# Attention values as the stationary operand, two key heads in column halves, in a hybrid trunk on one core

## The chip, the core and the metric

The kernel runs on one core of a Trainium2 chip. The metric is the device time of one execution in microseconds (us). The time of a kernel is the median of its runs; the profile is one further execution, with timestamps for the instructions of each engine. Engines: TensorE (PE) multiplies matrices, VectorE (DVE), ScalarE (ACT) and GpSimd (POOL) do elementwise work, and SyncE (SP) issues the DMAs. Matmuls read SBUF and write PSUM, which has eight banks of 128 partitions by 512 fp32 columns here.

## The reference

A trunk of two layers on 256 tokens of width 1024, all in fp32. Each layer has a feed-forward half step, a mixer, a second half step and a gated embedding. The mixer normalises x, multiplies it by one wide matrix `w_in`, and gives the columns to an mLSTM (four heads) and to a sliding-window attention (eight query heads on two key heads, 64 wide), whose outputs meet in two gated products:

```python
z = u @ w_in[i]
hA = mlstm_chunkwise(...)
yA = (jax.nn.sigmoid(mo) * rmsnorm(hA, ml_out_norm[i])) @ w_a[i]
pr = jnp.exp(logits - m)
denom = jnp.sum(pr, axis=-1, keepdims=True) + jnp.exp(sink - m)
hB = jnp.einsum('bnkgqs,bnskd->bnqkgd', pr / denom, vv)
yB = hB @ w_b[i]
mixed = jax.nn.sigmoid(ga) * yA + jax.nn.sigmoid(gb) * yB
x = x + mixed @ w_out[i]
```

## The kernel before

The tokens are two tiles of 128, called t = 0 and t = 1. Every weight is read once from HBM, in units of up to 128 x 2048 (`load_next`): one DMA into `raw` on SP's queue, then for each half of the unit a cast to `hi` on ACT (L203) and the rest `lo = raw - hi` on DVE (L204). Units are loaded three ahead of their use. A product of activations and weights is three matmuls of 512 columns each (`mm_unit`, L231 lo, L232 hi with the activations' lo, L233 hi), and the activations are split into `hi` and `lo` the same way (`split_evac`, L247 and L248 in the rows).

TensorE works in the order in which the code is written; the instructions of the other engines are put in order by a scheduler when the program is built. `stream` takes one unit, multiplies it with both token tiles (12 matmuls for each in `w_in`), and calls `tick()` after each tile. `tick()` advances every side task, a Python generator, by one step: so the attention, the mLSTM and the transposes are written between the units of a product. The counts W_... say how many steps a task waits.

The mixer multiplies `w_in` in nine pieces, sq, if, mqk, mv, mo, ga0, ga1, gb0, gb1 (`project`). Beside the last four of these run:

- `swa_logits` and `swa_part`: logits L, their exponentials (L694), the row sums rs and the reciprocal rinv (L699) of the softmax; then the transpose of L to PT. t = 0 has one part with all eight heads, t = 1 has two parts of four heads (`_1_0` and `_1_4`), as it sees 256 keys in two blocks kt.
- A transpose of this kind (`turn`) doesn't use TensorE: DVE transposes blocks of 32 x 32 (L264), a DMA writes the result to a scratch in HBM (L270, `scr`), a second one reads it back in another order (L274, `back`), and a copy puts it in its place (for PT: ACT at L709 for the first block of a part, DVE at L711 for the others). The `back` tile has two buffers, and PT, hb and ha all use them.
- the product of PT with the values `vsw` (L721), into `ov`: PT is the stationary operand (128 keys x 128 tokens), the values (128 keys x 64) move; one small matmul for each head and each kt, 8 for t = 0 and 16 for t = 1. The output has tokens on partitions. `hb = ov * rinv` (L729), then hb takes the same way over HBM to have its channels on partitions, and is split into `abT[t][1]`, which the rows call abT_1.
- `ml_mix` and `ml_out`: products st of the mLSTM's queries and keys (L807, L815; row halves of the array side by side), E times st on DVE (L811, L819), num (L838 for t = 0, L840 and L841 for t = 1) from E and its values, its denominator dd and r (L844, L845), ha = num * r (L846), squares on ACT (L850), vn and rn (L852, a power on POOL), the norm (L856), a sigmoid gate (ACT L881, DVE L862), and the way over HBM to `abT[t][0]`, abT_0.

After gb1 `drain()` lets every task end, and for each half n of the output columns `stream` multiplies abT_1 by `w_b` (yb) and abT_0 by `w_a` (ya): 24 matmuls each, t = 0 first. `by_cols` gives `w_b`'s half as one DMA: row 128 k + p of the matrix on partition p, k = 0 to 3, which matches hb's channels in order.

Of the kernel before, what the change touches and what calls it, by code (L numbers as in the profile page):

```python
# [8 lines left out]
F32 = mybir.dt.float32  # L9
# [5 lines left out]
P = 128  # L15
# [13 lines left out]
SWKV = 2  # L29
# [28 lines left out]
W_OV = 2  # L58
W_HB = 1
W_ST = 2  # L60
# [5 lines left out]
def trunk_kernel(ctx: ExitStack, tc: tile.TileContext, a: dict, out: bass.AP):  # L66
# [14 lines left out]
    def bank(name):  # L81
        return psum.tile([P, 512], F32, tag="bank", name=name)
# [34 lines left out]
    def by_cols(w, rows, cols, name):  # L117
# [13 lines left out]
        ]  # L131

    def by_rows(w, rows, name):
        return [
            (f"{name}_{k}", k, 2, [w[k * P : (k + 2) * P, :]], D) for k in range(0, rows // P, 2)
        ]
# [29 lines left out]
    for i in range(DEPTH):  # L166
        specs.extend(ffn_specs(a["ffn1_wi"][i], a["ffn1_wo"][i], f"f1{i}"))
        for z, cols in Z.items():
            specs.extend(by_cols(a["w_in"][i], D, cols, f"z{i}_{z}"))
        for n in range(2):  # L170
            cols = [(512 * n, 512 * (n + 1))]
            specs.extend(by_cols(a["w_b"][i], 512, cols, f"wb{i}_{n}"))
            specs.extend(by_cols(a["w_a"][i], 512, cols, f"wa{i}_{n}"))
        specs.extend(by_rows(a["w_out"][i], D, f"wout{i}"))
        specs.extend(ffn_specs(a["ffn2_wi"][i], a["ffn2_wo"][i], f"f2{i}"))
        specs.extend(by_rows(a["w_ple"][i], PDIM, f"wple{i}"))
        specs.extend(by_rows(a["w_ple_gate"][i], D, f"pg{i}"))
    loaded = deque()

    def load_next(between=()):  # L180
# [14 lines left out]
        else:  # L195
            c0 = 0
            for s in srcs:
                w = s.shape[1]
                nc.sync.dma_start(rv[:, :, c0 : c0 + w], s.rearrange("(k p) c -> p k c", p=P))
                c0 += w  # L200
# [316 lines left out]
    def mix_in(pool, i, xn, finish):  # L517
# [127 lines left out]
        def swa_logits(t):  # L645
# [6 lines left out]
            nh = SWQ if t == 0 else SWQ // SWKV  # L652
            parts = []
            for h0 in range(0, SWQ, nh):
                nmp = f"{i}_{t}_{h0}"
# [17 lines left out]
            for h0, L, mx in parts:  # L673
                gen = swa_part(t, h0, nh, L, mx)
                spawn(gen)
                advance(gen)

        def swa_part(t, h0, nh, L, mx):
            part = slice(h0, h0 + nh)
# [18 lines left out]
            rinv = stat("rinv")  # L698
            nc.vector.reciprocal(rinv, rs)  # L699
            for _ in range(W_PT):  # L700
                yield
# [11 lines left out]
            for _ in zip(*[turn_p(kt, j0) for kt in range(t + 1) for j0 in range(0, nh, 4)], strict=True):  # L713
                yield
            for _ in range(W_OV):
                yield
            ov = bank(f"ov{nmp}")[:, 0 : nh * HD]
            for j in range(nh):
                g = (h0 + j) // 4
                for kt in range(t + 1):  # L720
                    nc.tensor.matmul(  # L721
                        ov[:, j * HD : (j + 1) * HD],
                        PT[:, kt, j, :],
                        vsw[kt][:, g * HD : (g + 1) * HD],
                        start=kt == 0,
                        stop=kt == t,
                    )
            hb = work.tile([P, nh * HD], F32, tag="sg", name=f"hb{nmp}")
            nc.vector.tensor_tensor(  # L729
                heads(hb, HD), heads(ov, HD), rinv[:, :, None].broadcast_to([P, nh, HD]), op=ALU.mult  # L730
            )
            for _ in range(W_HB):
                yield
            ks = slice(h0 * HD // P, (h0 + nh) * HD // P)
            hi, lo = (part[:, ks, :] for part in abT[t][1])
            yield from back_split(blocks(hb), hi, lo, f"hb{nmp}")

# [313 lines left out]
```

## Time and profile before

| what | before |
|---|---|
| median of three runs | 1118.13 us (1116.99 to 1119.06) |
| the profiled execution, its own time | 1118.42 us |
| its span | 1116.6 us |
| DVE TENSOR_TENSOR lo_f, 128x1024, 176 times | 207.5 us busy, mean 1216 ns |
| PE matmuls h_f of 128x512, L232 | 352, 137.8 us busy, mean 392 ns |

The span runs from the first instruction to the last. A row of the timeline has the start in us, the duration in us, the engine, the line, the operation, output <- inputs, the shapes (output <- input), and how many instructions it stands for; a bracket says how long the engine sat idle ahead of it and what it waited for. Matmuls overlap in the pipeline, so their pace is read from start to start and not from the duration.

### The profile page before, as it was taken

The numbers are of one execution on the slowest core, as the hardware profiler recorded it, in microseconds if no ns is written. First come the engines' busy times: TensorE is split into PE (matmuls) and PEld (weight loads), VectorE is DVE, ScalarE is ACT, GpSimd is POOL, SyncE is SP. The second block draws the span as 40 slices with busy tenths as digits, with TensorE's granted clock in tenths as the row PEclk, the third lists the DMA queues.
The fourth block names the chain that finished last, engine by engine and source line by source line (L and its number), as shares of the span: only waits on it lengthen the run. The fifth ranks groups of instructions, "written<-read, shape, count | busy, mean of one in ns | idle before, by whom it ended". The sixth has DMA issues, their size and how long they took to land.

```text
span 1116.6 us, 13467 instructions
## 1 busy us (share of the span) xinstructions
PE 1104.3 (99%) x5096; PEld 913.7 (82%) x5096; DVE 756.7 (68%) x958; ACT 585.7 (52%) x848; POOL 29.6 (3%) x30
## 2 busy tenths in 40 slices
PE   8999999999999999999999999999999999999998
PEld 6788888878878888888888888888787888888887
DVE  5775655689787576656676666556987777667563
ACT  5543544668545444444664454446784454444442
POOL 1000000010000000000000000001000000000000
PEclk9999999999999999999999999999999999999999
DMA  7888766778764867766657776666777557777551
GB/s 252 282 268 255 258 212 191 244 229 264 241 212 156 274 228 254 247 202 221 215 164 246 261 231 224 214 206 211 254 249 243 198 185 245 244 238 247 194 207 38
DMA packets 170337, 251.30 MB, mean 225 GB/s; under 512 B 18472, under 2 KB 70816, under 8 KB 170272
## 3 DMA queue, kind: packets, MB, share of 16 engines
q1 hardware_dynamic: 170272, 250.44, 68.4%
q8 instruction: 40, 0.66, 0.2%
q14 instruction: 25, 0.20, 0.1%
HBM read 227.59 MB, written 22.83 MB: 224 GB/s over the span
## 4 chain that ended last, share of the span: by engine, by line
PE 80%; DVE 11%; DMA 4%; issue 2%; ACT 2%; POOL 1%; SPq 0%; DVEq 0%
PE h_f L232 14%; PE h_f L231 14%; PE h_f L233 14%; PE acc_f_o L232 7%; PE acc_f_o L233 7%; PE acc_f_o L231 7%; DMA back_PT<-scr_PT 2%; PE acc_wout L233 1%; PE acc_wout L231 1%; PE acc_wout L232 1%; PE acc_pg L233 1%; PE acc_pg L231 1%; PE acc_pg L232 1%; DVE lo_z_ga L204 1%; DVE inq_PT L264 1%
## 5 line engine op out<-in xcount | busy, mean ns | idle before, releaser
L204 DVE TENSOR_TENSOR lo_f<-raw_f,hi_f 128x1024 fp32r<-128x1024 f32 (+1 forms) x176 | 207.5, 1216 | 85.2 <-ACT hi_f L203 84.9
L203 ACT CAST hi_f<-raw_f 128x1024 fp32r<-128x1024 f32 (+1 forms) x178 | 176.5, 1038 | 143.8 <-PE h_f L233 88.1
L204 DVE TENSOR_TENSOR lo_f_o<-raw_f_o,hi_f_o 128x1024 fp32r<-128x1024 f32 x88 | 104.2, 1219 | 71.9 <-ACT hi_f_o L203 71.8
L232 PE MATMUL h_f<-hi_f,xT_f_0l 128*128 128x512 f32 x352 | 137.8, 392 | 2.2 <-DVE xT_f_0l L248 2.2
L231 PE MATMUL h_f<-lo_f,xT_f_0h 128*128 128x512 f32 x352 | 138.5, 393 | 0.2 <-POOL lo_f L204 0.2
L233 PE MATMUL h_f<-hi_f,xT_f_0h 128*128 128x512 f32 x352 | 137.7, 391 | 0.0
L231 PE MATMUL h_f<-lo_f,xT_f_1h 128*128 128x512 f32 x352 | 137.2, 390 | 0.5 <-DVE lo_f L204 0.4
L232 PE MATMUL h_f<-hi_f,xT_f_1l 128*128 128x512 f32 x352 | 137.0, 389 | 0.0
L233 PE MATMUL h_f<-hi_f,xT_f_1h 128*128 128x512 f32 x352 | 136.9, 389 | 0.0
L203 ACT CAST hi_f_o<-raw_f_o 128x1024 fp32r<-128x1024 f32 x88 | 88.0, 1048 | 90.0 <-PE acc_f_o L233 53.0
L232 PEld LDWEIGHTS h_f<-hi_f,xT_f_0l 128*128 128x128 f32 x352 | 66.4, 189 | 16.1 <-DVE xT_f_0l L248 2.5
L231 PEld LDWEIGHTS h_f<-lo_f,xT_f_1h 128*128 128x128 f32 x352 | 66.1, 188 | 15.1 <-DVE lo_f L204 1.4
L231 PEld LDWEIGHTS h_f<-lo_f,xT_f_0h 128*128 128x128 f32 x352 | 66.3, 188 | 14.7 <-issue 0.6
L233 PEld LDWEIGHTS h_f<-hi_f,xT_f_0h 128*128 128x128 f32 x352 | 66.5, 189 | 13.8
L233 PEld LDWEIGHTS h_f<-hi_f,xT_f_1h 128*128 128x128 f32 x352 | 66.1, 188 | 13.7
L232 PEld LDWEIGHTS h_f<-hi_f,xT_f_1l 128*128 128x128 f32 x352 | 66.0, 188 | 13.6
L233 PE MATMUL acc_f_o<-hi_f_o,hT_f_1h 128*128 128x512 f32 x176 | 68.5, 389 | 0.0
L231 PE MATMUL acc_f_o<-lo_f_o,hT_f_0h 128*128 128x512 f32 x176 | 68.5, 389 | 0.0
L232 PE MATMUL acc_f_o<-hi_f_o,hT_f_0l 128*128 128x512 f32 x176 | 68.5, 389 | 0.0
L233 PE MATMUL acc_f_o<-hi_f_o,hT_f_0h 128*128 128x512 f32 x176 | 68.5, 389 | 0.0
L231 PE MATMUL acc_f_o<-lo_f_o,hT_f_1h 128*128 128x512 f32 x176 | 68.5, 389 | 0.0
L232 PE MATMUL acc_f_o<-hi_f_o,hT_f_1l 128*128 128x512 f32 x176 | 68.5, 389 | 0.0
(355 smaller groups left out, 2033.0 us busy)
## 6 DMA issues: line engine op xcount, KB each, us to landing
raw_f<-in_ffn_wi_dram SPq DMA_DIRECT2D x79, 1024.0 KB, 5.5
raw_f_o<-in_ffn_wo_dram SPq DMA_DIRECT2D x40, 1024.0 KB, 5.4
scr_h_f<-inq_h_f SPq DMA_DIRECT2D x40, 256.0 KB, 4.2
back_h_f<-scr_h_f SPq DMA_DIRECT2D x40, 256.0 KB, 3.7
raw_f<-in_ffn_wi_dram SPq DMA_DIRECT2D x18, 512.0 KB, 4.6
raw_z_ga<-in_w_in_dram SPq DMA_DIRECT2D x8, 1024.0 KB, 5.5
raw_z_gb<-in_w_in_dram SPq DMA_DIRECT2D x8, 1024.0 KB, 7.6
raw_wout<-in_w_out_dram SPq DMA_DIRECT2D x8, 1024.0 KB, 5.1
```

The costliest lines, as they stand in the source:

```text
L203: nc.scalar.copy(hi[:, o:e], raw[:, o:e])
L204: (nc.gpsimd if between and o // step % 2 == 0 else nc.vector).tensor_tensor(lo[:, o:e], raw[:, o:e], hi[:, o:e].bitcast(F32), op=ALU.subtract
L231: nc.tensor.matmul(o, xh, wl[:, k, sl], start=start, stop=False)
L232: nc.tensor.matmul(o, xl, wh[:, k, sl], start=False, stop=False)
L233: nc.tensor.matmul(o, xh, wh[:, k, sl], start=False, stop=stop)
L264: nc.vector.transpose(inq[:, 0:n].rearrange(f"p (b {order}) -> p b k s", b=4, k=k), src.rearrange("p k (c b) -> p b k c", b=4),)
```

## The change

The values become the stationary operand: for key head g and key block kt, the 64 columns of `vsw[kt]` that belong to g stand in one column half of the array, and the four query heads of g with their 128 tokens, 512 columns of PT, move. The two key heads write to the partitions 0 to 63 and 64 to 127 of one bank, so the output has channels on partitions already: partition 64 g + d, column block j for head 4 g + j. It is split from PSUM into abT_1 without a trip over HBM. L is multiplied by rinv before it is transposed (in place, 128 x 1024, once for t = 0 and twice for t = 1), in place of hb's product. At t = 1 each of the two parts appends its PT to a list `turned`, and only the second part goes on to the product. `w_b` is read so that its rows match: rows 256 g + 64 j + d on partition 64 g + d, in two DMAs of 64 partitions for each half (`by_heads`).

```diff
@@ -56,7 +56,6 @@
 W_MB = 2
 W_PT = 3
 W_OV = 2
-W_HB = 1
 W_ST = 2
 W_NUM = 1
 W_HA = 3
@@ -130,6 +129,11 @@
             for k in range(0, kt, step)
         ]
 
+    def by_heads(w, cols, name):
+
+        c0, c1 = cols
+        return [(f"{name}_0", 0, 4, [w[256 * g : 256 * (g + 1), c0:c1] for g in range(SWKV)], c1 - c0)]
+
     def by_rows(w, rows, name):
         return [
             (f"{name}_{k}", k, 2, [w[k * P : (k + 2) * P, :]], D) for k in range(0, rows // P, 2)
@@ -169,7 +173,7 @@
             specs.extend(by_cols(a["w_in"][i], D, cols, f"z{i}_{z}"))
         for n in range(2):
             cols = [(512 * n, 512 * (n + 1))]
-            specs.extend(by_cols(a["w_b"][i], 512, cols, f"wb{i}_{n}"))
+            specs.extend(by_heads(a["w_b"][i], cols[0], f"wb{i}_{n}"))
             specs.extend(by_cols(a["w_a"][i], 512, cols, f"wa{i}_{n}"))
         specs.extend(by_rows(a["w_out"][i], D, f"wout{i}"))
         specs.extend(ffn_specs(a["ffn2_wi"][i], a["ffn2_wo"][i], f"f2{i}"))
@@ -194,8 +198,12 @@
                 also()
         else:
             c0 = 0
-            for s in srcs:
+            for g, s in enumerate(srcs):
                 w = s.shape[1]
+                if s.shape[0] < kk * P:
+                    rows = slice(HD * g, HD * (g + 1))
+                    nc.sync.dma_start(rv[rows, :, :], s.rearrange("(k p) c -> p k c", p=HD))
+                    continue
                 nc.sync.dma_start(rv[:, :, c0 : c0 + w], s.rearrange("(k p) c -> p k c", p=P))
                 c0 += w
         for o in range(0, n, step):
@@ -651,6 +659,7 @@
             per = 512 // nk
             nh = SWQ if t == 0 else SWQ // SWKV
             parts = []
+            turned = []
             for h0 in range(0, SWQ, nh):
                 nmp = f"{i}_{t}_{h0}"
                 L = pool.tile([P, nh, nk], F32, tag="s4", name=f"L{nmp}", bufs=4)
@@ -671,11 +680,11 @@
                     nc.vector.tensor_tensor(L[:, js, :], os[g], bias[:, head : head + per, boff:], op=ALU.add)
                     nc.vector.reduce_max(mx[:, js], L[:, js, :], axis=AX.X)
             for h0, L, mx in parts:
-                gen = swa_part(t, h0, nh, L, mx)
+                gen = swa_part(t, h0, nh, L, mx, turned)
                 spawn(gen)
                 advance(gen)
 
-        def swa_part(t, h0, nh, L, mx):
+        def swa_part(t, h0, nh, L, mx, turned):
             part = slice(h0, h0 + nh)
             nmp = f"{i}_{t}_{h0}"
 
@@ -697,6 +706,7 @@
             nc.vector.tensor_tensor(rs, rs, es, op=ALU.add)
             rinv = stat("rinv")
             nc.vector.reciprocal(rinv, rs)
+            nc.vector.tensor_tensor(L, L, rinv[:, :, None].broadcast_to([P, nh, L.shape[2]]), op=ALU.mult)
             for _ in range(W_PT):
                 yield
             PT = pool.tile([P, t + 1, nh, P], F32, tag="s4", name=f"PT{nmp}", bufs=4)
@@ -712,28 +722,21 @@
 
             for _ in zip(*[turn_p(kt, j0) for kt in range(t + 1) for j0 in range(0, nh, 4)], strict=True):
                 yield
+            turned += [PT[:, :, j0 : j0 + 4, :] for j0 in range(0, nh, 4)]
+            if len(turned) < SWKV:
+                return
             for _ in range(W_OV):
                 yield
-            ov = bank(f"ov{nmp}")[:, 0 : nh * HD]
-            for j in range(nh):
-                g = (h0 + j) // 4
-                for kt in range(t + 1):
+
+
+            ov = bank(f"ov{i}_{t}")
+            for kt in range(t + 1):
+                for g in range(SWKV):
+                    rows = slice(g * HD, (g + 1) * HD)
                     nc.tensor.matmul(
-                        ov[:, j * HD : (j + 1) * HD],
-                        PT[:, kt, j, :],
-                        vsw[kt][:, g * HD : (g + 1) * HD],
-                        start=kt == 0,
-                        stop=kt == t,
+                        heads(ov, P)[rows], vsw[kt][:, rows], turned[g][:, kt], start=kt == 0, stop=kt == t
                     )
-            hb = work.tile([P, nh * HD], F32, tag="sg", name=f"hb{nmp}")
-            nc.vector.tensor_tensor(
-                heads(hb, HD), heads(ov, HD), rinv[:, :, None].broadcast_to([P, nh, HD]), op=ALU.mult
-            )
-            for _ in range(W_HB):
-                yield
-            ks = slice(h0 * HD // P, (h0 + nh) * HD // P)
-            hi, lo = (part[:, ks, :] for part in abT[t][1])
-            yield from back_split(blocks(hb), hi, lo, f"hb{nmp}")
+            split_evac(*abT[t][1], blocks(ov))
 
 
         cem = small.tile([P, 16], F32, tag="cem", name=f"cem{i}")
```

The change moves instructions on several engines. On TensorE, the rows around the attention product of t = 1 (`ov_1...`; `z_mix_gb` is the product with the columns gb0 of w_in, `PT_1_0` and `PT_1_4` are the two parts). Before, the last of the sixteen:

```order
L721 MATMUL ov_1_4_2448<-vsw_1_1556,PT_1_4_2182 128x64
L721 MATMUL ov_1_4_2448<-vsw_0_1555,PT_1_4_2182 128x64
L721 MATMUL ov_1_4_2448<-vsw_1_1556,PT_1_4_2182 128x64
L231 MATMUL z_mix_gb_1_2413<-lo_z_gb_0_2191,xT_mix_1_0h 128x512
L232 MATMUL z_mix_gb_1_2413<-hi_z_gb_0_2190,xT_mix_1_0l 128x512
```

and of the change, at the same place:

```order
L241 MATMUL z_mix_gb_0_2409<-hi_z_gb_0_2193,xT_mix_0_0h 128x512
L736 MATMUL ov_1_2431<-PT_1_0_2178,vsw_0_1555 64x512
L736 MATMUL ov_1_2431<-PT_1_4_2185,vsw_0_1555 64x512
L736 MATMUL ov_1_2431<-PT_1_0_2178,vsw_1_1556 64x512
L736 MATMUL ov_1_2431<-PT_1_4_2185,vsw_1_1556 64x512
L239 MATMUL z_mix_gb_1_2410<-lo_z_gb_0_2194,xT_mix_1_0h 128x512
```

The product stands between the same two units; four wide matmuls replace sixteen narrow ones, and the second and the fourth read PT_1_4.

On VectorE, the rows around the products of E with st, ahead of num (`inq_PT` are the transposes of L, `lo_z` the splits of weights). Before:

```order
L264 STREAM_TRANSPOSE inq_PT_1_0_1_0_2179<-L_1_0_2042 128x512
L204 TENSOR_TENSOR lo_z_ga_4_2118<-raw_z_ga_4_2116,hi_z_ga_4_2117 128x1024 x2
L264 STREAM_TRANSPOSE inq_PT_1_4_0_0_2183<-L_1_4_2044 128x512
L264 STREAM_TRANSPOSE inq_PT_1_4_1_0_2186<-L_1_4_2044 128x512
L811 TENSOR_TENSOR E_0_2143<-E_0_2143,st_0_2217 128x2x128
L811 TENSOR_TENSOR E_0_2143<-E_0_2143,st_1_2218 128x2x128
L811 TENSOR_TENSOR E_0_2143<-E_0_2143,st_0_2217 128x2x128
L811 TENSOR_TENSOR E_0_2143<-E_0_2143,st_1_2218 128x2x128
L819 TENSOR_TENSOR E_0_2144<-E_0_2144,st_0_2227 128x128
```

and of the change:

```order
L212 TENSOR_TENSOR lo_z_ga_4_2121<-raw_z_ga_4_2119,hi_z_ga_4_2120 128x1024
L709 TENSOR_TENSOR L_1_4_2045<-L_1_4_2045,rinv_1_4_2096 128x1024
L212 TENSOR_TENSOR lo_z_ga_4_2121<-raw_z_ga_4_2119,hi_z_ga_4_2120 128x1024
L272 STREAM_TRANSPOSE inq_PT_1_0_0_0_2179<-L_1_0_2043 128x512
L272 STREAM_TRANSPOSE inq_PT_1_0_1_0_2182<-L_1_0_2043 128x512
L814 TENSOR_TENSOR E_0_2146<-E_0_2146,st_0_2220 128x2x128
L814 TENSOR_TENSOR E_0_2146<-E_0_2146,st_1_2221 128x2x128
L814 TENSOR_TENSOR E_0_2146<-E_0_2146,st_0_2220 128x2x128
L212 TENSOR_TENSOR lo_z_gb_0_2194<-raw_z_gb_0_2192,hi_z_gb_0_2193 128x1024 x2
L814 TENSOR_TENSOR E_0_2146<-E_0_2146,st_1_2221 128x2x128
L822 TENSOR_TENSOR E_0_2147<-E_0_2147,st_0_2230 128x128
```

The scalings of L stand ahead of the transposes, a pair of weight splits has moved ahead of the fourth product, and the transposes of PT_1_4 have moved behind it; they come four and six rows below the last one shown.

On VectorE again, the last copy of PT (`ha` is the mLSTM's output, `vn` and the four products at its norm). Before:

```order
L846 TENSOR_TENSOR ha_1_2238<-num_1_0_2355,r_1_2352 128x256
L846 TENSOR_TENSOR ha_1_2238<-num_1_1_2366,r_1_2352 128x256
L711 COPY PT_1_4_2182<-back_PT_1_4_1_0_2187 128x512
L852 TENSOR_SCALAR vn_0_2317<-ssn_0_2297 128x4
L856 SCALAR_TENSOR_TENSOR ha_0_2237<-ha_0_2237,rn_0_2319,mlg_1551 128x128 x4
L862 TENSOR_TENSOR ha_0_2237<-ha_0_2237,gates_0_1559 128x512
L729 TENSOR_TENSOR hb_0_0_2408<-ov_0_0_2399,rinv_0_0_2013 128x512
```

and of the change:

```order
L849 TENSOR_TENSOR ha_1_2241<-num_1_1_2369,r_1_2355 128x256
L855 TENSOR_SCALAR vn_0_2320<-ssn_0_2300 128x4
L859 SCALAR_TENSOR_TENSOR ha_0_2240<-ha_0_2240,rn_0_2322,mlg_1551 128x128 x4
L865 TENSOR_TENSOR ha_0_2240<-ha_0_2240,gates_0_1559 128x512
L721 COPY PT_1_4_2185<-back_PT_1_4_1_0_2190 128x512
L855 TENSOR_SCALAR vn_1_2380<-ssn_1_2356 128x4
L272 STREAM_TRANSPOSE inq_ha_0_2438<-ha_0_2240 128x512
```

The copy that fills the last block of PT_1_4 stood ahead of the norm of ha (t = 0) and now stands behind its six instructions.

## Prediction

> **What bounds the kernel now.** I read the page's busy shares first, then the waits of TensorE, then a table by windows over the stages that the change touches. The page's first lines:
>
> ```profile
> span 1116.6 us, 13467 instructions
> ...
> PE 1104.3 (99%) x5096; PEld 913.7 (82%) x5096; DVE 756.7 (68%) x958; ACT 585.7 (52%) x848; POOL 29.6 (3%) x30
> ```
>
> TensorE (PE) is busy through 99% of the span. So an edit is worth only what it takes from the time that matmuls hold PE, or from PE's few stops. The profiled run took 1118.42 us, 1.8 of it around the span, and stands 0.29 above the median of 1118.13; my sum starts from 1118.42. The waits (engine, line, waited for: us in all, times, longest) name two stops at the product with w_b:
>
> ```profile
> PE yb L232 <- DVE abT_1l L248: 1.2, 2, 1.0
> PE yb L231 <- ACT abT_1h L247: 1.1, 1, 1.1
> ```
>
> Both wait for abT_1, the attention output after its trip through HBM. Their full price is more than the 2.3 us here, so I took windows (us, PE busy, PEld, DVE, ACT, POOL, then granted clock, DMA share, GB/s): 72 matmuls without a stop in layer 0, the first 48 of yb and ya in layers 0 and 1, and two pieces of the last.
>
> ```profile
> 288.49:304.81 16.32, 16.32 (x74) 13.52 (x72) 12.21 (x16) 6.62 (x9) 0.00 (x0) 1.00 0.81 258
> 304.81:317.54 12.73, 12.18 (x50) 8.78 (x49) 9.77 (x12) 7.77 (x11) 0.00 (x0) 1.00 0.72 235
> 852.68:867.83 15.15, 13.08 (x50) 10.06 (x48) 10.48 (x13) 8.80 (x12) 0.00 (x0) 0.89 0.67 227
> 855.30:858.70 3.40, 1.33 (x5) 0.67 (x4) 3.03 (x4) 3.18 (x7) 0.00 (x0) 1.00 0.22 58
> 858.70:862.10 3.40, 3.40 (x10) 2.61 (x9) 2.73 (x3) 1.58 (x2) 0.00 (x0) 0.50 0.90 312
> ```
>
> 16.32/72 is 0.2267 us a matmul, so 48 should take 10.88. Layer 0 loses 12.73 - 10.88 = 1.85 and layer 1 loses 15.15 - 10.88 = 4.27, together **6.12 us**. The last two rows show why layer 1 loses more: after 3.40 us in which PE worked only 1.33, its clock was granted at 0.50 for the next 3.40, which costs half of that, 1.7.
>
> **What goes: the trip of hb.** The product hb, its transposes, its way to HBM and back, and W_HB are gone; ov now leaves PSUM straight into abT_1. The split of the last ov can start when it ends, near 287, while yb starts at 304.81: it is not late by some 17 us. The returns of hb also shared two `back` buffers with those of ha, and the last of ha stood behind them; that queue goes too. So I take off all 6.12. What is late next at yb is its weights:
>
> ```profile
> 294.13 2.35 DVE L204 TENSOR_TENSOR lo_wb<-raw_wb,hi_wb 128x1024 fp32r<-128x1024 f32 x2
> ```
>
> They are split at 296.5, 8.3 us ahead of yb. That cover hides the load in two halves on 64 partitions each; beyond 8.3 us of delay it costs PE its full excess. I price it at nothing.
>
> **What the attention product costs on PE.** Before, 16 and 32 records (an fp32 matmul shows as two):
>
> ```profile
> 277.62 1.89 PE L721 MATMUL ov<-vsw,PT 128*128 128x64 f32 x16
> 279.32 0.48 PE L231 MATMUL z_mix_gb<-lo_z_gb,xT_mix_0h 128*128 128x512 f32 x1
> ...
> 282.16 3.68 PE L721 MATMUL ov<-vsw,PT 128*128 128x64 f32 x32
> 285.65 0.48 PE L231 MATMUL z_mix_gb<-lo_z_gb,xT_mix_0h 128*128 128x512 f32 x1
> ```
>
> Start to start, token tile 0 holds PE 1.70 us, tile 1 3.49. The new form is two matmuls of 512 columns, then four. An fp32 matmul that wide isn't in the trace; the widest is:
>
> ```profile
> 50.85 0.48 PE L490 MATMUL relb<-onehot,rb 32*8 32x384 f32 x1
> 51.17 0.48 PE L490 MATMUL relb<-onehot,rb 32*8 32x384 f32 x1
> ```
>
> Two records of 384 columns start 0.32 apart, 0.83 ns a column, so 512 columns take 0.427 a record and 0.85 a matmul. Two halves of the array can work together, if they are halves by rows:
>
> ```profile
> 259.32 0.39 PE L233 MATMUL z_mix_ga<-hi_z_ga,xT_mix_1h 128*128 128x512 f32 x1
> 259.63 1.14 PE L807 MATMUL st<-qkT 64*128 64x256 f32 x8
> 260.60 0.61 PE L815 MATMUL st<-qkT 64*128 64x128 f32 x8
> 261.14 0.50 PE L231 MATMUL z_mix_ga<-lo_z_ga,xT_mix_1h 128*128 128x512 f32 x1
> ```
>
> Four matmuls of 256 columns would take 4 x 0.427 = 1.71 one after another; they took 0.97, side by side. With the 128-column ones (half of that, 0.48) streaming is 1.45 of the 1.51 from 259.63 to 261.14, and the first starts 0.08 late after 259.32 + 0.227. I allow 0.3 for entry and exit. For halves by columns the bounds are 1.15 and 2.01 (side by side) and 2.01 and 3.72 (one after another, 0.85 more for each pair). I take the first, by the rows of st: 0.55 less at tile 0 and 1.48 less at tile 1, 2.03 a layer if nothing waits.
>
> [...]
>
> **What comes: VectorE ahead of the E products.** Three products per layer (L by rinv, 128x1024, one for tile 0, two for tile 1) now stand on VectorE (DVE) ahead of the transposes. Before:
>
> ```profile
> 262.38 2.33 DVE L204 TENSOR_TENSOR lo_z_ga<-raw_z_ga,hi_z_ga 128x1024 fp32r<-128x1024 f32 x2
> 264.61 2.12 DVE L264 STREAM_TRANSPOSE inq_PT<-L 128x512 f32<-128x512 f32 x2
> 266.63 1.39 DVE L811 TENSOR_TENSOR E<-E,st 128x256 f32<-128x256 f32 x4
> 267.92 0.50 DVE L819 TENSOR_TENSOR E<-E,st 128x128 f32<-128x128 f32 x2
> 268.31 2.37 DVE L204 TENSOR_TENSOR lo_z_gb<-raw_z_gb,hi_z_gb 128x1024 fp32r<-128x1024 f32 x2
> ```
>
> These stand close together: DVE has no slack here. The scaling isn't in the trace. Below it lies a copy (two of 128x512 at 0.43, 0.86); above it hb's product with the same broadcast operand (285.55 below, 0.68, two of them 1.36). The nearest is the subtraction of equal size, 2.28 a pair, and I take 1.14. The fourth E product ended at 266.63 + 1.39 = 268.02. Now three scalings (+3.42) and the pair lo_z_gb (+2.28) stand ahead of it, and two transposes (2.02) behind: it ends near 271.7. TensorE needs it here:
>
> ```profile
> 269.44 1.05 PE L838 MATMUL num<-vaug,E 128*128 128x129 f32 x8
> ```
>
> The fourth head comes after six of these eight records, at most 0.79 in, by 270.2. So PE, which did not stop here, **waits 1.5 us** now, and all that is queued on it, the z_mix units and then ov, comes 1.5 later. Tile 0's ov starts near 279.1 and takes 1.15; after twelve more matmuls, tile 1's ov is reached at 277.62 + 1.5 + 1.15 + 12 x 0.2267 = 283.0.
>
> **The last copy of PT.** That is not when it ends, since its last matmul needs PT_1_4 and the copy of it is moved behind ha's norm on DVE. Before:
>
> ```profile
> 280.19 0.76 DVE L846 TENSOR_TENSOR ha<-num,r 128x256 f32<-128x256 f32 x2
> 282.14 0.43 DVE L711 COPY PT<-back_PT 128x512 f32<-128x512 f32 x1 [1.19 <-DMA back_PT<-scr_PT]
> 282.48 0.16 DVE L852 TENSOR_SCALAR vn<-ssn 128x4 f32<-128x4 f32 x1
> 283.77 1.14 DVE L856 SCALAR_TENSOR_TENSOR ha<-ha,rn,mlg 128x128 f32<-128x128 f32 x4 [1.12 <-POOL rn L302]
> 284.94 0.69 DVE L862 TENSOR_TENSOR ha<-ha,gates 128x512 f32<-128x512 f32 x1
> 285.55 0.68 DVE L729 TENSOR_TENSOR hb<-ov,rinv 128x512 f32<-128x512 f32 x1
> ```
>
> I lay these durations along the new order, from the fourth product at 271.7: E2's products 0.8, two transposes 2.0, a pair lo_z_gb 2.3, PT_0's copy 0.35, another pair with the small ones of dd 2.5, r 0.1, ha's pair 0.7. That is 280.4, its first half 280.0. Then ScalarE (ACT) squares ha:
>
> ```profile
> 278.29 1.06 ACT L881 ACTIVATE gates<-gates 128x1024 f32<-128x1024 f32 x1
> ...
> 282.33 0.31 ACT L850 ACTIVATE jn<-ha 128x128 f32<-128x128 f32 x1
> 282.54 0.19 ACT L850 ACTIVATION_READ_ACCUMULATOR jn<-ha 128x1 f32 x1
> 282.76 0.31 ACT L850 ACTIVATE jn<-ha 128x128 f32<-128x128 f32 x1
> ```
>
> Four squares at 0.43, a sigmoid of 1.0 and two short ones of 0.1 each end at 282.9, where vn starts. By the rows above, vn to L856 is 1.29 (the power on GpSimd inside), L856 1.17, L862 0.61, and the copy 0.4: 286.4. The last matmul's 0.85 and 0.1 of exit bring z_mix back at 287.4, where it was 285.65: **+1.7 a layer**. It includes the 1.5 at num, since everything after it hangs on the same DVE chain, and it swallows the 2.03 that ov saves. What could be later than the copy is its data:
>
> ```profile
> DMA to landing us min/median/max: 2.8/3.8/5.5
> ```
>
> Its return can be issued when PT_1_0's copy frees a `back` buffer, near 280.8; at the median it lands at 284.6, at the worst at 286.3, so it sets nothing by 1.4 us at the median. Layer 1 runs the same order, and I take it alike.
>
> **The sum:** 1118.42 + 2 x 1.7 - 6.12 = **1115.7 us**, 0.24% below the profiled run. A measurement of this kernel can tell about 0.2%, 2.2 us, from no change: the bounds are 1115.9 and 1120.4.
>
> **The rivals.**
> - *DVE gives way.* If the scheduler's order costs PE nothing (a cheaper scaling and waits that fall into gaps), only the savings stay: 1118.42 - 2 x 2.03 - 6.12 = 1108.2. Against it stands that the E products' rows leave no gap; even at 0.86 a scaling the fourth product ends at 270.8 and PE waits. Chance 0.12.
> - *The clock falls after the new stops.* 855.30:858.70 shows that 1.33 us of work in 3.40 was too little. The new stops are near 1.5 each, so PE works about 1.9 of 3.40: not so little, but no row shows where the edge lies. Each fall costs 1.7: one gives 1117.4, one a layer 1119.1. Chance 0.16. [...]
> - *Column halves one after another*, so that the change doesn't pack as it says. Each pair costs 0.85 more, but tile 0 still comes before the copy and at tile 1 only the last pair's share shows, some 0.4 a layer: 1116.5, inside my range.
> - *Slower: the broadcast scaling at half pace.* It stands on the DVE chain three times a layer, so each 0.1 us of it costs 0.6 in all. At twice the subtraction, 2.24, that is 6 x 1.1 = 6.6: 1122.3. It decides from 1.14 + (1120.4 - 1115.7)/6 = 1.92 us a scaling. Against it is hb's row with its broadcast at 0.68. Chance 0.11.
>
> **How the numbers follow.** My forecast, with the third rival inside, has 0.61 and its own range is 1113.5 to 1117.5 (scalings of 0.86 to 1.36 take off 1.7 or add 1.3). With the falling clock above and half the way to the first rival below, the range is 1111.5 to 1119.6; outside lie that rival's rest and the last. Faster by over 0.2%: 0.39 of my forecast's chance and 0.12, 0.51. Within: 0.22 and 0.16, 0.38. Slower: 0.11.
>
> **What would show it.** Right: no wait of yb on abT_1; 48 matmuls of yb and ya in 10.9 to 11.3 us in both layers; a new stop of some 1.5 us at num on E; ov of tile 1 ending with a stop on PT from DVE; scalings of 1.1 to 1.2. Wrong: no stop at num (then the first rival), a row at 0.50 behind num or ov (the second), ov records of one pair starting 0.85 apart (the third), scalings near 2 us (the last).

## The result, and the profile after

The changed kernel is slower. Its median is 1125.06 us (15 runs, 1119.28 to 1127.79), against 1118.22 us (15 runs, 1116.25 to 1123.24) for the kernel before, timed beside it. The ratio is 1.0052, with a 95% interval of 1.0040 to 1.0064. The profiled execution took 1120.85 us. From here on L0 and L1 are the two layers.

The page's first lines, as shown of before:

```profile
span 1119.0 us, 13289 instructions
...
PE 1100.7 (98%) x5024; PEld 902.8 (81%) x5024; DVE 757.3 (68%) x950; ACT 585.9 (52%) x846; POOL 29.7 (3%) x30
```

TensorE does less work, 3.6 us less than the 1104.3 of before, in a span that is 2.4 longer: it stands still somewhere. Its waits (line, waited for: us in all, times, longest) say where:

```profile
PE ov L736 <- ACT PT L719: 5.7, 2, 3.0
PE num L841 <- DVE E L814: 2.7, 2, 1.3
```

The waits of yb on abT_1 are gone, as forecast, and so is what they cost. Windows of the first 48 matmuls of yb and ya, both layers (columns as in the prediction):

```profile
307.38:318.26 10.88, 10.88 (x50) 9.01 (x48) 7.31 (x8) 4.58 (x5) 0.00 (x0) 1.00 0.58 194
859.30:870.18 10.88, 10.88 (x49) 9.01 (x48) 7.31 (x8) 4.58 (x5) 0.00 (x0) 1.00 0.58 191
```

These are the 10.88 us of an undisturbed pace, where before took 12.73 and 15.15. Two stops took their place, one at num, which was forecast, and a longer one at ov of t = 1, and they cost more than that. The timeline of TensorE at ov:

```profile
277.08 1.08 PE L736 MATMUL ov<-PT,vsw 128*64 128x512 f32 x4
278.09 0.50 PE L239 MATMUL z_mix_gb<-lo_z_gb,xT_mix_0h 128*128 128x512 f32 x1
...
281.04 1.07 PE L736 MATMUL ov<-PT,vsw 128*64 128x512 f32 x2
284.88 3.40 PE L736 MATMUL ov<-PT,vsw 128*64 128x512 f32 x6 [2.77 <-ACT PT L719]
288.21 0.50 PE L239 MATMUL z_mix_gb<-lo_z_gb,xT_mix_0h 128*128 128x512 f32 x1
```

At t = 0 four records (two matmuls) hold TensorE 1.01 us, where two at the 0.85 us worked out in the prediction would take 1.70 one after the other: the column halves do work side by side. At t = 1 the first matmul starts at 281.04, the second, in the other column half, has to wait until 284.88, and z_mix comes back 7.17 us after the first. Before it took 3.49.

Since the two profiled executions differ by 2 us in their first 16 us (before's clock was granted at 0.50 from 12.21 to 15.62, the changed kernel's at 1.00 there), the layers are compared from a common mark: first starts in the timeline, from st of a layer to its second yb. Everything else agrees to 0.01 us (489.97 and 489.96 us from the second yb of L0 to st of L1, and 244.33 in both from the second yb of L1 to the last matmul). In all tables below, **A** is from num of t = 0 to num of t = 1, **B** from ov of t = 1 to the first yb, and **S** the whole, from st to the second yb:

| kernel | A, L0 / L1 | B, L0 / L1 | yb to yb, L0 / L1 | S, L0 / L1 |
|---|---|---|---|---|
| before | 3.65 / 3.65 | 22.65 / 22.65 | 12.73 / 15.15 | 57.90 / 60.32 |
| changed | 5.23 / 5.25 | 26.34 / 27.44 | 10.88 / 10.88 | 60.85 / 61.97 |

So the change costs 2.95 us in L0 and 1.65 in L1, 4.60 in all. The profiled executions differ by only 2.43, because the changed one began its first st 2.22 us sooner; the medians differ by 6.8.

Why ov is late is read on VectorE (DVE), with the chain of waits beside it. DVE's timeline in L0:

```profile
254.30 1.23 DVE L709 TENSOR_TENSOR L<-L,rinv 128x1024 f32<-128x1024 f32 x1
...
263.63 2.12 DVE L272 STREAM_TRANSPOSE inq_PT<-L 128x512 f32<-128x512 f32 x2
265.67 1.04 DVE L814 TENSOR_TENSOR E<-E,st 128x256 f32<-128x256 f32 x3
266.63 2.35 DVE L212 TENSOR_TENSOR lo_z_gb<-raw_z_gb,hi_z_gb 128x1024 fp32r<-128x1024 f32 x2
268.90 0.41 DVE L814 TENSOR_TENSOR E<-E,st 128x256 f32<-128x256 f32 x1
269.24 0.68 DVE L822 TENSOR_TENSOR E<-E,st 128x128 f32<-128x128 f32 x3
270.50 1.11 DVE L272 STREAM_TRANSPOSE inq_PT<-L 128x512 f32<-128x512 f32 x1 [0.59 <-DMA scr_PT<-inq_PT]
...
274.97 0.44 DVE L721 COPY PT<-back_PT 128x512 f32<-128x512 f32 x1
...
280.42 0.43 DVE L721 COPY PT<-back_PT 128x512 f32<-128x512 f32 x1 [1.66 <-DMA back_PT<-scr_PT]
...
286.12 0.42 DVE L721 COPY PT<-back_PT 128x512 f32<-128x512 f32 x1
```

and the chain of waits there (start us, us, what), followed back from ov:

```profile
264.78 5.62 DMA scr_PT<-inq_PT
...
270.50 0.59 DVE inq_PT L272
...
273.69 5.59 DMA back_PT<-scr_PT
...
284.32 0.52 ACT PT L719
```

Three things are to be seen. PT_1_0 is transposed at 263.63, and its two blocks fill both `inq` buffers, so PT_1_4's first transpose, at 270.50, waits until the write of PT_1_0 has landed. PT_1_0's own return stands behind PT_1_4's write on SP's queue, and goes out at 273.69 only. And the copy at 274.97, the second block of PT_0, 17.56 us after st where the kernel before has it 11.35 after st, holds one of the two `back` buffers until 275.4, so that PT_1_0's second return can't go out sooner either. The twelve returns of PT land 2.6 to 6.2 us after their issue, 4.0 at the median, and PT_1_4's two need the `back` buffers that PT_1_0's copies free (280.42 on DVE), so all that is late goes through two rounds of copies and returns. The last copy on ScalarE (ACT) starts at 284.23, the one on DVE at 286.12, behind ha's norm. How much of the latter is late data can be read from its return, the last of `back_PT`:

```profile
280.88 0.36 SPq L282 DMA_DIRECT2D back_PT<-scr_PT  x1
DMA to landing us min/median/max: 4.3/4.3/4.3
```

It landed near 285.2, 27.7 us after st, where the kernel before has it 22.5 after st; in L1 it is 27.3 against 23.3. So the data is 5.2 and 4.0 us later than before, and the place behind the norm adds 1.0 and 1.6 more.

And when TensorE goes on, it is slow:

```profile
281.04:284.88 3.84, 1.07 (x3) 0.19 (x3) 2.04 (x10) 3.71 (x16) 1.01 (x1) 0.94 0.92 237
284.88:288.21 3.33, 3.33 (x7) 0.58 (x7) 3.19 (x9) 3.33 (x7) 1.01 (x1) 0.55 0.23 47
```

After 3.84 us with 1.07 of work, the clock was granted at 0.55 in the mean of the second window: 0.50 from 284.45 to 287.86.

### The profile page after: what moved, and what is told of

Read it like the earlier page. It is cut to its first block, busy times and chain, and to the rows that moved or that the text cites. A ratio compares the mean times of both kernels' runs of the same rounds, so it can differ in the third digit from the quotient of the medians.

```text
span 1119.0 us, 13289 instructions
## 1 busy us (share of the span) xinstructions
PE 1100.7 (98%) x5024; PEld 902.8 (81%) x5024; DVE 757.3 (68%) x950; ACT 585.9 (52%) x846; POOL 29.7 (3%) x30
## 4 chain that ended last, share of the span: by engine, by line
PE 84%; DVE 7%; ACT 3%; DMA 3%; issue 2%; POOL 1%; SPq 0%; DVEq 0%; ACTq 0%
PE h_f L239 14%; PE h_f L241 14%; PE h_f L240 14%; PE acc_f_o L240 7%; PE acc_f_o L241 7%; PE acc_f_o L239 7%; PE acc_wout L241 1%; PE acc_wout L239 1%; PE acc_wout L240 1%; PE acc_pg L239 1%; PE acc_pg L240 1%; PE acc_pg L241 1%; PE z_mix_gb L239 1%; PE z_mix_gb L240 1%; PE z_mix_gb L241 1%
```

## The experiments

Each is the changed kernel with one edit, except e8. The table holds the spans of all; two numbers in a field are L0 / L1. **C** is when PT's last copy ends, after the first st of its layer; a stop at ov depends on C and on where ov stands on TensorE. The ratio is to the kernel before, run on the same chip.

| run | A | B | C | S | median us (runs) | ratio, 95% interval |
|---|---|---|---|---|---|---|
| before | 3.65 / 3.65 | 22.65 / 22.65 | 22.9 / 23.8 | 57.90 / 60.32 | | |
| changed | 5.23 / 5.25 | 26.34 / 27.44 | 29.1 / 29.3 | 60.85 / 61.97 | 1125.06 (15) | 1.0052 (1.0040 to 1.0064) |
| e1_unscaled | 3.65 / 3.64 | 21.57 / 22.44 | 23.4 / 24.2 | 54.49 / 55.36 | 1110.07 (4) | 0.9918 (0.9892 to 0.9944) |
| e2_own_buffers | 5.56 / 3.98 | 21.08 / 21.08 | 24.3 / 23.8 | 59.15 / 57.55 | 1117.00 (10) | 0.9987 (0.9973 to 1.0002) |
| e3_fill | 5.26 / 5.23 | 26.18 / 25.74 | 29.5 / 29.0 | 60.62 / 60.15 | 1120.50 (10) | 1.0020 (1.0006 to 1.0034) |
| e4_ov_later | 5.23 / 5.23 | 15.64 / 15.64 | 29.4 / 29.2 | 55.59 / 55.59 | 1110.91 (4) | 0.9933 (0.9913 to 0.9954) |
| e5_pool | 5.34 / 5.33 | 22.51 / 21.57 | 28.0 / 27.2 | 59.12 / 58.25 | 1116.84 (10) | 0.9994 (0.9985 to 1.0004) |
| e6_inq | 3.99 / 6.50 | 22.91 / 21.08 | 28.3 / 27.3 | 59.41 / 60.08 | 1117.86 (10) | 0.9997 (0.9986 to 1.0009) |
| e7_num_ov_later | 3.65 / 3.65 | 17.75 / 16.91 | 30.4 / 29.6 | 56.12 / 55.27 | 1111.52 (6) | 0.9945 (0.9931 to 0.9959) |
| e8_before_hb_buffers | 3.65 / 3.65 | 22.65 / 22.65 | 23.1 / 23.8 | 56.48 / 59.86 | 1115.42 (10) | 0.9986 (0.9973 to 0.9999) |
| e9_later_still | 3.65 / 3.65 | 12.92 / 12.92 | 30.7 / 30.4 | 54.00 / 54.00 | 1108.12 (5) | 0.9903 (0.9889 to 0.9918) |
| e10_back | 5.26 / 5.26 | 22.59 / 22.31 | 25.2 / 24.9 | 57.12 / 56.84 | 1113.45 (4) | 0.9951 (0.9933 to 0.9969) |
| e11_copies_first | 4.45 / 4.46 | 26.52 / 23.27 | 28.9 / 27.0 | 61.36 / 58.10 | 1122.05 (5) | 1.0045 (1.0021 to 1.0069) |
| e12_inq_copies_first | 5.07 / 5.32 | 21.08 / 21.08 | 25.4 / 24.1 | 58.96 / 59.20 | 1117.74 (10) | 1.0006 (0.9993 to 1.0018) |

**e1: no scaling.**

```diff
-            nc.vector.tensor_tensor(L, L, rinv[:, :, None].broadcast_to([P, nh, L.shape[2]]), op=ALU.mult)
```

> The changed kernel without the product of L by rinv: the attention's probabilities stay undivided, so this output isn't the reference's. Two stages are read in the trace: A, from num of t=0 to num of t=1 (3.64 us before, 5.24 after), and B, from ov of t=1 to yb (22.65 before; 26.34 and 27.44 after in the two layers; 21.1 without any stop). Theory 1 (the three scalings of some 1.15 us on VectorE make both stops, since everything behind them there comes later): A 3.6, B 21 to 22, time some 14 us below the changed kernel, near 1110. Theory 2 (the scalings are only a small part; the stop at ov comes from PT's transfers over HBM, whose buffers and places in SP's queue the new order of the code made worse): A 3.6, but B stays at 24 or more, time near 1117.

The stop at num is gone (A is 3.65), and of the one at ov little is left: B is 21.57 and 22.44, where 21.08 is the time without a stop (e2, below). So the scalings set both off. This kernel leaves out the division by the softmax's sums, and nothing else. The scalings take 3 x 1.14 us of DVE a layer (254.30 to the next instruction at 255.44), and their absence is worth 6.4 and 6.6 us of S: nearly twice their own time. Without them DVE's order, too, is that of before.

**e2, e6 and e10: buffers of their own for PT_1_4.** e6 gives them to the transposes (`inq`), e10 to the returns (`back`), e2 to both, each in the room of a tile that is no longer read.

```diff
-            inq = work.tile([P, 5 * P], F32, tag="xg", name=f"inq_{name}")
-            back = pool.tile([P, 5 * P], F32, tag="back", name=f"back_{name}", bufs=2)
+            last = name.startswith("PT") and name.split("_")[1:3] == ["1", "4"]
+            kt = name.split("_")[3] if last else "0"
+            if last:
+                if not inq14:
+                    inq14.append(pool.tile([P, 2, 512], F32, tag="qkT", name=f"inq_{name}"))
+                inq = inq14[0][:, int(kt)]
...
+            if last:
+                back = pool.tile([P, 4, P], F32, tag=f"qTs{kt}", name=f"back_{name}").rearrange("p k c -> p (k c)")
...
```

> The scalings stay; the transposes of PT_1_4 and its returns get buffers of their own, in the room of tiles that are no longer read (qkT, and the queries' qTs). VectorE's order then has PT_1_4's transposes and a pair of weight splits ahead of all four E products. Theory 1 (VectorE's load by the scalings): A grows to about 7, as two transposes more stand ahead of the E products, and B stays above 25. Theory 2 (buffers and SP's queue in PT's transfers): A grows the same, but B falls to 21 to 23, since the returns no longer wait for one another.

> Half of e2: only the transposes of PT_1_4 get a buffer of their own, its returns share the two back buffers again. If what made the stop at ov is that PT_1_4's transposes wait for the write of PT_1_0 (5.6 us from issue to landing in the chain of waits of the changed kernel) and hold back PT_1_0's return on SP's queue: B falls as in e2, 21 to 22.5. If it is the returns that wait for PT_1_0's copies (back has two buffers): B stays at 24 to 25. The stop at num is as in e2 in both cases, since VectorE's order ahead of the E products is the same.

> The other half of e2: only the returns of PT_1_4 have buffers of their own; its transposes share the two of PT_1_0 again, so A and the order ahead of the E products are as in the changed kernel (A 5.2). If the shared returns are a second part of the stop at ov (in the changed kernel the return of PT_1_4 is issued at 280.0, when PT_1_0 has been copied, and lands near 284), B falls by about 2 to 4, to 22 to 24. If only the late transposes count, B stays at 26.

B is 21.08 in e2: no stop at all, since 84 matmuls at 0.2267 are 19.04 and 2.04 is left for ov itself. But B alone misleads here. Free to run at once, PT_1_4's transposes stand ahead of all E products in e2 and e6, in e2's timeline of DVE:

```profile
265.88 4.06 DVE L272 STREAM_TRANSPOSE inq_PT<-L 128x512 f32<-128x512 f32 x4
269.87 2.32 DVE L212 TENSOR_TENSOR lo_z_gb<-raw_z_gb,hi_z_gb 128x1024 fp32r<-128x1024 f32 x2
272.10 1.41 DVE L826 TENSOR_TENSOR E<-E,st 128x256 f32<-128x256 f32 x4
```

so num waits longer, and num of t = 0 starts 3.2 us later after st than in the changed kernel. (I had expected that growth in A; it stands ahead of A, as num's first matmul waits already.) With num, ov stands later, and part of its stop has only moved. C tells them apart. The returns' buffers (e10) take 4 us off C, from 29.1 and 29.3 to 25.2 and 24.9, and S falls by 3.7 and 5.1. The transposes' buffer (e6) takes off 0.9 and 2.0, and its B of 21 to 23 was no success of that theory. Both (e2) take off 5. In e2 and e10 the scheduler also put the last copies ahead of the norm, so C has both effects in it. But in e10 DVE's last copy still waits for its data (0.30 us, in L0) and ends 4.1 us sooner, while its place behind the norm made only 1.0 us in the changed kernel: most of the gain is the data's. e6's queue on SP shows what was left:

```profile
267.00 3.30 SPq L278 DMA_DIRECT2D scr_PT<-inq_PT  x4
272.22 0.38 SPq L207 DMA_DIRECT2D raw_z_gb<-in_w_in_dram  x1
272.91 4.39 SPq L282 DMA_DIRECT2D back_PT<-scr_PT  x2
```

The write of PT_1_4 is out early, so are the first of PT_1_0's returns, at 272.91, and yet the second goes out 4.0 us later, 17.3 after st: PT_0's copy ends just then and frees a `back` buffer.

**e11 and e12: PT's copies first.** e11 gives them the scheduler's high priority, which moves PT_0's second copy up among the E products; e12 is e11 and e6 together.

```diff
-                if kt + j0 == 0:
-                    nc.scalar.copy(dst, b)
-                else:
-                    nc.vector.tensor_copy(dst, b)
+                with tc.high_priority():
+                    if kt + j0 == 0:
+                        nc.scalar.copy(dst, b)
+                    else:
+                        nc.vector.tensor_copy(dst, b)
```

> The copies of PT get the scheduler's high priority. In the order of the instructions this moves one thing of weight: PT_0's second copy on VectorE stands among the E products, where the changed kernel has it behind the transposes of PT_1_4 and two more pairs of splits (it starts 17.56 us after st there, 11.35 in the kernel before). PT_0's copy frees one of the two back buffers, so the second return of PT_1_0 has to wait for it: 18.03 after st in the changed kernel, 13.13 before. The ends of PT's last copies, after st, are 27.4 and 29.1 in the changed kernel, 22.4 and 22.9 before. If only this late copy makes the returns late: PT_1_0's second return at 13 to 14, the last copies at 24 to 25, B near 22.5. If the write of PT_1_4 ahead of it on SP's queue counts as well: the second return goes out near 16.8, a little over 1 us sooner, and the last copies end 1 to 1.5 sooner, near 28, B 25.

> e6 and e11 together: PT_1_4's transposes have a buffer of their own, so its write leaves SP's queue early, and PT_0's second copy stands early, so the back buffer is free; the returns still share two buffers. e6 alone moved the last copies by 0.9 us only (26.5 and 28.3 after st): its second return of PT_1_0 waited until 17.3 for PT_0's copy. If the stop at ov is made by these two together, either of which holds back the return of PT_1_0: its two returns go out near 13.3 and 13.8 after st, its copies end by 19, PT_1_4's last copies near 23.5, as in the kernel before, and ov does not wait (B 21.1), with the stop at num as in e6 (num of t=0 some 13 after st). If the shared back buffers alone make it, whatever stands ahead: the last copies stay at 26 to 28.

In e11 PT_1_0's second return goes out 16.5 and 16.1 us after st, where SP's queue lets it, and C falls by 0.2 and 2.4: the second of the two cases, with L0 less than expected. (Num of t = 0 starts 1.1 us later after st than in the changed kernel, so S grows by 0.5 in L0.) In e12 both obstacles are gone, and SP's queue has the returns in two quick pairs:

```profile
271.42 1.02 SPq L282 DMA_DIRECT2D back_PT<-scr_PT  x2
272.49 0.50 SPq L207 DMA_DIRECT2D raw_z_gb<-in_w_in_dram  x1
276.75 0.91 SPq L282 DMA_DIRECT2D back_PT<-scr_PT  x2
```

The first pair goes out 13.4 us after st (257.98), PT_1_0's copies end by 18.7, and C is 25.4 and 24.1, near what two private returns gave in e10, though 23.5 was expected. Ov does not wait, but num waits 3.4 us in each layer, so the time stays at that of the kernel before. So PT_1_0's return is held twice, by PT_1_4's write and by PT_0's copy, and either alone holds it.

**e3: work in the stop.**

```diff
+            for _ in range(10 * t):
+                nc.tensor.matmul(ov[:, 0:P], ones, ones, start=True, stop=True)
```

> Ten matmuls of ones by ones (128x128, overwritten afterwards) stand ahead of the attention product of t=1, in its own bank: about 2.2 us of work in a place where TensorE stands still for 3.0 us in the changed kernel. Clock theory (the stop halves TensorE's clock for the next 3.4 us, in this profile once a layer, and more often in the slower of the 15 runs, whose mean clock falls from 0.998 to 0.992 as the time rises from 1119.3 to 1126.4): no window of half clock behind ov, B about 25.5 in both layers, 0.9 and 1.9 less, and times nearer together, 1118 to 1121. Rival (the clock has no part in it): B equal or longer, and the same spread.

The clock holds. The windows of the changed kernel at the same times, in this run:

```profile
281.04:284.88 3.84, 3.34 (x23) 2.34 (x21) 1.80 (x9) 3.71 (x18) 1.01 (x1) 1.00 0.81 207
284.88:288.21 3.33, 2.30 (x7) 0.61 (x8) 3.21 (x9) 3.33 (x7) 1.01 (x1) 1.00 0.36 86
```

Work without any use makes the kernel faster, 1120.50 us at the median. In the profile B wins 1.70 in L1, about as expected, but only 0.16 in L0, where the slow matmuls had run inside the wait for the last copy on DVE (286.12 + 0.42) anyway. Over all runs the clock weighs more: the mean clock that stands with each of the changed kernel's runs falls from 0.998 at 1119.28 us to 0.992 at 1126.39, and e3's runs lie between 0.997 and 1.0. By the falls in the profiles of the two kernels, 3.41 us at 0.50 each, one costs 1.7 us and 0.0015 of the mean (1.7 of 1120); so I estimate 0.006 less as four falls, 6.8 us, where 7.1 were measured. (The slowest run, 1127.79, stands at 0.992 too, so this is a rough count.) Which stops have them in the runs without a trace is open. The times did not draw as near together as expected: 1117.96 to 1122.70.

**e5: the scalings on GpSimd.**

```diff
-            nc.vector.tensor_tensor(L, L, rinv[:, :, None].broadcast_to([P, nh, L.shape[2]]), op=ALU.mult)
+            nc.gpsimd.tensor_tensor(L, L, rinv[:, :, None].broadcast_to([P, nh, L.shape[2]]), op=ALU.mult)
```

> The three scalings of L run on GpSimd in place of VectorE; nothing else is edited. The span read is st to the second yb (57.90 and 60.32 before, 60.85 and 61.97 after in the two layers, 54.49 and 55.36 without any scaling, 54.0 without any stop). Theory 1 (the scalings' time on VectorE starts both stops): A back to 3.65, B 21.1 to 23 (GpSimd is slower at such a product, so PT comes later by the difference), span 54 to 56, time about 1110. Theory 2 (buffers of PT's transfers alone): the order of the transfers and their two buffers are as before the change, so it expects the same or a B of 23 to 25 where GpSimd's scaling takes over 2 us.

A miss for the first theory in the form that I gave it. S falls by 1.7 and 3.7 only, since the stop at num stays. GpSimd's timeline in L0, and a DVE row beside it:

```profile
256.70 1.98 POOL L709 TENSOR_TENSOR L<-L,rinv 128x1024 f32<-128x1024 f32 x1 [29.62 <-issue]
262.23 3.75 POOL L709 TENSOR_TENSOR L<-L,rinv 128x1024 f32<-128x1024 f32 x2 [3.55 <-DVE rs L706]
```

```profile
256.84 2.39 DVE L797 TENSOR_TENSOR E<-Mb,maskb 128x512 f32<-128x512 f32 x1
```

It takes 1.88 to 1.98 for what DVE does in 1.14, the transposes behind wait for it, and while it ran a sum on DVE that takes 0.66 in the changed kernel (257.77 there) took 2.39. What matters is how late the scaled L is, on whichever engine: C is 28.0 and 27.2, and a good part of B's fall to about 22 is again that num, and ov behind it, stand later (num of t = 0 by 2.0).

**e4, e7 and e9: the waiting matmuls stand later.**

```diff
-W_OV = 2
-W_NUM = 1
+W_OV = 4
+W_NUM = 2
```

e4 has only W_OV = 4, e7 both as shown, e9 W_OV = 5 and W_NUM = 2.

> W_OV is 4 in place of 2: the attention product comes two units of 12 matmuls later on TensorE, 5.4 us. If the stop at ov is only a matter of where it stands, the span from num of t=1 to yb (31.73 before, 34.93 and 36.03 after) falls to 29.7, and the time to about 1112, with A unchanged at 5.2. Rival (the copies are late because VectorE and ScalarE are behind, and stay behind whatever TensorE does): the stop moves with it or comes back at the end of the stage, the span stays above 32.

> W_OV 4 as in e4, and W_NUM 2 in place of 1: num also comes one unit of 12 matmuls later on TensorE. If both stops are only a matter of where the waiting matmuls stand, none is left: the span from st to the second yb falls from 55.59 in e4 to 54.0 in both layers, and the time to about 1107.5. Rival: the mLSTM's output ha comes 2.7 us later and ya waits for it; then the span from the first to the second yb grows above 10.88.

> W_NUM 2 as in e7 and W_OV 5: e7 had no stop at num left, but still waited 1.1 us at ov, as the last copy of PT on VectorE had moved behind still more work. With ov yet later no stop should be left: the span from st to the second yb 54.0 in both layers (56.12 and 55.27 in e7, 55.59 in e4), the time near 1107.5. Rival: the attention's split of abT_1, or ha behind the later num, is late for yb or ya; then the span from the first to the second yb is above 10.88.

In e4 nothing on DVE, ACT or the queues is faster (C is 29.4 and 29.2); ov only stands two units later on TensorE, and its stop is gone. S is 55.59 in both layers, which leaves the 1.6 of num. In e7 num's stop is gone too, but the late num pushes the last copies behind more work, and ov waits again (1.1 us at most), so e7 is no better than e4. In e9 no stop is left, as the window from st to the second yb shows for L0:

```profile
257.51:311.51 54.00, 54.00 (x257) 42.96 (x257) 42.39 (x72) 38.66 (x74) 2.95 (x2) 1.00 0.78 234
```

TensorE is busy through all 54.00 us; S in L1 is the same. With 1108.12 us (1106.48 to 1108.87) e9 beats both kernels.

**e8: the kernel before, with hb's returns in buffers of their own.**

```diff
+            if name.startswith("hb"):
+                spare = 1 if name.split("_")[1:] == ["1", "0"] else 0
+                back = pool.tile([P, 4, P], F32, tag=f"qTs{spare}", name=f"back_{name}").rearrange("p k c -> p (k c)")
...
```

> The kernel before, with one edit: hb's returns get buffers of their own, in the room of the queries' qTs, and don't share the two of ha. If the stops at yb and ya in the kernel before come from this sharing, the span from the first to the second yb falls from 12.73 and 15.15 to 10.9 and 11 without any change to the attention, the time to about 1112. If they come from the length of hb's trip itself (product, transpose, write, read), they stay above 12 and 14 and only the change removes them.

From yb to yb it is 11.31 and 14.68, so 1.42 of 1.85 come back in L0, and 0.47 of 4.27 in L1. In L1 TensorE still waits, and its clock still falls:

```profile
PE yb L232 <- DVE abT_1l L248: 1.0, 1, 1.0
PE yb L231 <- ACT abT_1h L247: 0.7, 1, 0.7
```

```profile
850.91:854.32 3.41, 1.78 (x7) 0.95 (x6) 3.23 (x5) 3.41 (x8) 0.00 (x0) 1.00 0.83 311
854.32:857.73 3.41, 3.41 (x10) 2.63 (x9) 2.87 (x4) 1.86 (x2) 0.00 (x0) 0.50 0.90 308
```

The second row is a fall of the clock and costs 1.7, as it did before the change. So of the 4.42 us that the stops themselves cost in both layers (6.12 less 1.7), the sharing makes 1.89, most of it in L0; the change takes away the rest too. That the rest is the length of hb's trip is likely from the waits on abT_1, but no run tests it alone.

## Why the prediction was wrong

- **The forecast** was 1115.7 us, faster, with a range to 1119.6. The measured 1125.06 is outside it, on the other side.
- **What goes** held to the hundredth: 6.12 us at yb and ya are gone in the changed kernel, and e8 shows that buffers for hb's returns would have given back only 1.89 of them. Some luck is in it: 1.7 of the 6.12 were one fall of the clock in L1 of one profile, and a longer stop, of 3.05 us in L1 of e2, brought none (last section).
- **The product on TensorE** held: 1.01 us at t = 0 (1.15 forecast), and 2.04 at t = 1 where nothing waits (2.01). The halves by columns run side by side (1.01 us for two matmuls, against 1.70 one after the other), as the rows of st show it for halves by rows (0.97 against 1.71), so that rival falls.
- **The scaling** held: 1.14 us each, the value taken. The rival that made the kernel slower by this price falls, though e1 shows that the scalings do start the loss. So the kernel is slower for a reason that no rival had.
- **The stop at num** held: A grew by 1.58 and 1.60, 1.5 was forecast.
- **The step that failed** is the one on the last copy of PT, the term "+1.7 a layer". Measured, from st to the first yb, it is +4.79 (49.97 against 45.18) and +5.91, 10.70 in place of 3.4 in the sum. I had said of its data that "it sets nothing by 1.4 us at the median", counting from PT_1_0's copy near 280.8. Num started at 269.44 before and at 267.21 in the changed run, so 2.23 has to be added to its times: PT_1_0's copy on DVE ended at 280.42 + 0.43 + 2.23 = 283.1. It was 2.3 late, as it waited for its own return, which I had not followed. I laid DVE's order out, and even had PT_0's copy in it some 6 us later than before, but did not ask for what it frees: the `back` buffer of PT_1_0's second return. Nor did I look at the `inq` buffers, which hold PT_1_4's transposes until PT_1_0 is written, or at SP's queue, where PT_1_0's return stands behind PT_1_4's write. e6, e11 and e12 show that the return is held by both, and e10 that two more buffers for PT_1_4's returns take 4 us off the last copy. Nor had I laid out the copy on ACT, that of PT_1_4's first block, which ended at 284.84, behind squares of ha, and let TensorE go on only then. DVE's last copy ended at 286.54 + 2.23 = 288.8, against 286.4. Of these 2.4 us its data made 1.4 (landed at 285.2 + 2.23 = 287.4, where the copy was to start at 286.0), and waiting behind the norm for its turn on DVE the other 1.0. So the sentence that the data sets nothing was wrong, and the norm was later than laid out as well: vn started at 283.06 + 2.23 = 285.3 against 282.9, with DVE's 1.66 us of wait for PT_1_0's return ahead of it.
- **The falling clock** was a rival at 0.16, priced at 1.7 for each fall. It came about, and its place is behind ov: e3, with 3.34 us of work in the 3.84 of the stop where the changed kernel has 1.07, kept the clock at 1.00 in the next window, where that has 0.55. I had weighed it for stops of 1.5 us; the stop became 3.84, with 3.0 as its longest wait. The last section has the windows ahead of other falls.
- **The other rival**, in which only the savings stay, was priced at 1108.2 us with the scheduler's order as its reason. The price was right: e9 gives 1108.12, and its S is 10.22 below that of the kernel before where the rival had 10.18. The reason was not: nothing on DVE gives way there, the waiting matmuls just stand where their data is ready.

The sum closes so: in the changed kernel S is 122.82 over both layers, and 108.00 without stops (e9). Of the 14.82 between, the stop at num is 3.18 (e4 less e9) and that at ov 11.64 (the changed kernel less e4), of which 2.05 come back when TensorE is given work there (e3). Before has 118.22, so the savings are 10.22, and 14.82 - 10.22 is the loss of 4.60. The rest of the 6.8 between the medians goes with the lower mean clock of the other runs; no trace shows in which stops.

## What to carry to other kernels

When work is moved ahead of a transfer's first step, the new order has to be laid out on every queue that the transfer passes, its buffers with it, and not only on the engine that got the work. Of every copy that moves, ask which buffer it frees, and who waits for that: two shared buffers made one late copy count twice. In a stream whose order is written by hand, the cheaper answer to a late operand is often to let its consumer stand later: here two constants turned 0.5% slower into 1.0% faster.

## What was not expected of the hardware

TensorE's clock fell behind windows in which TensorE had been at work for part of the time; in e5 for nearly half of it:

```profile
269.21:272.62 3.41, 1.60 (x12) 1.18 (x11) 3.41 (x8) 3.39 (x4) 0.00 (x0) 1.00 0.89 215
272.62:276.03 3.41, 3.41 (x10) 2.64 (x10) 3.41 (x7) 2.19 (x6) 0.00 (x0) 0.50 0.93 273
```

Ahead of this fall TensorE stood idle for 1.81 us of 3.41 in sum. It was 1.63 in e8 (850.91:854.32, shown above, where the longest single wait was 1.0), 2.07 in L1 of the kernel before (855.30:858.71) and 2.34 and 2.33 in the changed one (281.04:284.45 and 834.00:837.41); these last three falls were to 0.50, for 3.41 us each. But a stop of about the same length brought a fall or not. The stop at num of 3.07 us in L0 of e2 brought one, with 0.80 in 272.00:275.40 and 0.69 in 275.40:278.80; its stop of 3.05 us in L1 none, with 1.00 from 817.00 to 830.60. In e6, whose two stops at num are 6.1 us together, the longer 3.1, it was the other way round: 1.00 from 268.60 to 278.80 in L0, and in L1 0.59, 0.50 and 0.90 in the three windows of 3.40 from 820.40 on. What tells these stops apart is left open here. The stop of 1.3 us at num alone, in e4, showed no fall: the mean clock of its profiled run is 1.0.

And beside a product on GpSimd a sum on VectorE took 2.39 us, where it takes 0.66 in the changed kernel, in both layers, and its start and end lie with GpSimd's: it began 0.14 after GpSimd's row in L0 and 0.10 in L1, and 256.84 + 2.39 is 0.55 after GpSimd's end at 258.68. Stream transposes beside a later GpSimd product were not lengthened (264.16, two in 2.11 us, in e5's timeline; two in 2.12 at 263.63 in the changed kernel's).
